# A table of places where a step's first instruction stands behind another step, an earlier copy of two columns, and one moved down unit, in a hybrid attention and convolutional-MLP layer

## The chip, the cores and the metric

The kernel runs on one NeuronCore of a Trainium2 chip. Its engines each take their instructions in the order of their own queue: TensorE (PE: matmuls and, apart, weight loads), VectorE (DVE), ScalarE (ACT), GpSimd (POOL) and SyncE (SP), which issues most of the DMAs. The metric is the device time of one execution in microseconds (us); of several executions the median counts.

## The reference

One decoder layer on x of 1024 rows by 1024 columns, in float32:

```python
h = rms_norm(x, mix_norm)
z = h @ w_in            # gq, gk, gv, gr, glr (group A), sq, sk, sv (group B)
o_gla = gla_chunked(...)            # chunked gated linear attention, 4 heads
o_gla = rms_norm(o_gla, gla_norm) * silu(gr)
o_swa = swa_sink_attention(...)     # window of 128, 8 query heads, sinks
x = x + concatenate([o_gla, o_swa]) @ w_out
h2 = rms_norm(x, ffn_norm)
u = causal_dwconv(h2 @ w_up, conv_w, conv_b)   # 3 taps, 2 x 2816 channels
a, bval = split(u, 2)
return x + (silu(a) * bval) @ w_down
```

## The kernel before

**Tiles and numbers.** The 1024 rows are 8 tiles of 128. A float32 operand is held as two parts in a type that TensorE takes at full rate, a high part (a cast, on ACT) and a low part (source minus high part, on DVE or POOL), and each product runs three passes: high by high, high by low, low by high.

**Stages.** First come the dense products with w_in by tile: queries (`dq`), keys with the gate's low-rank input (`dk`), values (`dv`), gla queries and keys (`dg`), the output gate (`dr`), all by `dense` (L389). Beside them run the two attentions. For each tile, `kvl_tr` (L475, L476) transposes the keys and the gate's input (`kpt`); ACT copies the transposed gate input to `gt`, and `kvl_la` multiplies it (`za`, L493). `swa_scores` (L525, L526) makes the window's scores (`sc`). `unit_v` ends in an ACT copy into `vg` (L920). `load_piece` brings a piece of w_in by DMA (`graw` for the g weights) and casts it in two halves (`gw`, L116). Then comes the product with w_out (`oP`, L867), the second norm, its transposes (`n2_tr`, L264) into PSUM banks `n2pt` or `fb`, and then the MLP: 22 chunks of 128 + 128 channels up (`product`, L1033), the convolution, and the way down (`dn_P`, L1214, summed into `acc` by DVE, L1218).

**Up products.** The product with w_up is a Strassen-like scheme: seven products P1 to P7 per chunk instead of eight, with weights A11, A12, S1 to S4, A22 and with operands B11, B21, B22, T1 to T4, which are halves of the transposed rows and sums of them. P1 takes A11, P2 takes A12, P3 takes S4, P5 takes S1, P6 takes S2. A product is 12 matmuls of 128x512. The sums are made in the PSUM banks of the transposes (`n2_sum`, L285 to L293) and cut into high part (`n2_part_hi`, ACT L303) and low part (`n2_part_lo`, DVE L307). The last chunks' rows of the way down go the same way by pairs of chunks: a pair has seven sums (`down_g`), 14 units of 6 matmuls (`down_pair`).

**PSUM.** Pool `psa` has four banks. The transposes of tile 6 (`n2pt_6_0`) and the up products of chunk 1 and later (`fb0` to `fb3`) share them in turn: the bank that chunk 1's P2 writes is the one that held `n2pt_6_0`, which is free only when its last reader is through. That is step `l.T4.6` in the list `STEPS`, the low part of T4 of tile 6, the last but one entry (DVE, L307).

**What sets the order.** Steps are entered with a time (`at`, `at_us`) and emitted by that time. A scheduler then orders each engine's instructions. In the stretch from the w_out product to the MLP, manual dependencies that carry no wait (`NoSync`) pin PE's instructions to the order of emission, and in its second half those of DVE, ACT and POOL too; `STEPS` is the order written out by hand for that half. Before and after that stretch the scheduler decides: chunk 0's P3, P5 and P6 come after it, and the scheduler may put them between pinned ones. A wait between engines is a semaphore.

**MLP steps.** `post` calls `c11` when P2 of a chunk is done: DVE adds P1's copy, then `conv` runs an ACT activation (first tap and bias, L1045) and two DVE taps (L1040), and `save_edge` copies the last two columns for the second half (ACT, `e`, L1089). `down_pair` units stand between products: none up to (2, 0), one behind each product up to (21, 0), then two.

Of the kernel before, what the change touches and what calls it, by code (L numbers as in the profile page):

```python
# [27 lines left out]
NPAIR = NCH // 2 - 1  # L28
# [13 lines left out]
wl.0.A22 h.T4.5 T4a.6 T4b.6 wl.0.S3 tr.7.0 copy.1 tr.7.1 b12.7 up.1.P2 l.T4.5 h.B22.7 T1.7 h.T4.6 l.B22.7  # L42
h.T1.7 T3.7 l.T1.7 h.T3.7 l.T3.7 T2.7 T4a.7 h.T2.7 T4b.7 l.T2.7 h.T4.7 l.T4.6 l.T4.7
""".split()
PASSES = ((0, 0), (0, 1), (1, 0))
HALF = (slice(0, 64), slice(64, 128))

# [2 lines left out]
def hymba_layer_kernel(ctx, tc, x, mix_norm, w_in, w_alpha2, b_alpha, gla_norm,  # L50
                       q_norm, k_norm, sinks, w_out, ffn_norm, w_up, conv_w,
                       conv_b, w_down, out):
    nc = tc.nc
# [985 lines left out]
    def tap(dst, src, w):  # L1039
        dve.scalar_tensor_tensor(dst, src, w, dst, op0=ALU.mult, op1=ALU.add)  # L1040

    def conv(ch, sd, u, y, a, z, fresh):
        ci = sd * NCH + ch
        w0, w1, w2, b = (cc[:, i, ci:ci + 1] for i in range(4))
        act.activation(u[:, a:z], y[:, a:z], AF.Identity, bias=b, scale=w2)  # L1045
        a1, a2 = (a + 1, a + 2) if fresh else (a, a)
        tap(u[:, a1:z], y[:, a1 - 1:z - 1], w1)
        tap(u[:, a2:z], y[:, a2 - 2:z - 2], w0)
# [38 lines left out]
    def save_edge(ch, key, pb):  # L1087
        e = psb[key, ch] = base.tile([P, 2], F32, tag="e", name=f"{key}_{ch}", bufs=2)
        act.copy(e, pb[:, 510:512])  # L1089

    def c11(ch):
        pb = psb["P2", ch]
        dve.tensor_add(pb, psb["p1", ch], pb)  # L1093
        ua = psb["ua", ch] = wide_tile(f"ua{ch}", "ua")
        conv(ch, 0, ua, pb, 0, 512, True)
        save_edge(ch, "e", pb)

    def c12(ch):
        pb, ua = psb["P3", ch], psb["ua", ch]
# [237 lines left out]
    for t in range(NT):  # L1337
        if t > 1:
            if t > 3:
                at(t - 2.7, load_x, t)  # L1340
                at(t - 2.5, norm1, t)
                at(t - 1.6, lambda tt=t: norm_tr(tt, xts["h", tt], "n1"))
            if t > 2:
                at(TQ + t, unit_q, t)
        at(TK + 0.6 * t, unit_k, t)
        at(TK + 0.6 * t + 1.9, kvl_tr, t)
        at(TK + 0.6 * t + 3.1, kvl_la, t)
        at(TV + t, unit_v, t)
        at(TG + t, unit_g, t)
        at(TR + t, unit_r, t)  # L1350
        if t < 4:
            at(TR + 2.05 + 0.01 * t, load_acc, t)
        else:
            at(O + 2.25 + 0.005 * t, load_acc, t)
# [110 lines left out]
    for ch, i, name in order:  # L1465
        starts[ch, i] = tu
        prods.append((ch, name, tu))
        at_us(tu, product, ch, name)
        tu += MM
        at_us(tu - 0.1, post_last if ch == L else post, ch, name)  # L1470
        if (ch, name) == (0, "P4"):
            at_us(tu - 0.05, post, 1, "P2")
        if ch < 2 or (ch, i) == (2, 0):
            n = 0
        elif ch < L - 1 or (ch, i) == (L - 1, 0):
            n = 1
        else:
            n = 2
        for _ in range(n):
            if units:  # L1480
                unit = units.pop(0)
                unit_at[unit] = tu
                at_us(tu, down_pair, *unit)
                tu += UNIT
# [9 lines left out]
    for p in range(NPAIR):  # L1494
        for k in range(7):

            n = 7 * p + k - 2
            t0 = unit_at[n // 7, n % 7, 1] + UNIT if n >= 0 else starts[1, 4 + k] if k == 0 else starts[2, 0]
            at_us(t0 + 0.02, down_w, p, k)
            at_us(t0 + 0.03, down_g, p, k)  # L1500
        for i in range(2):
            if p == 0:
                t0 = starts[1, 2 + i]
# [11 lines left out]
    for t in range(NT):  # L1515
        at_us(tu, last_row, t)
        tu += MM
    last, PINNED = {}, (mybir.EngineType.DVE, mybir.EngineType.Activation, mybir.EngineType.Pool)
    for time, _, f, a in sorted(ev, key=lambda e: e[:2]):
        n = len(nc.cur_bb.bb.instructions)  # L1520
        f(*a)
        if O <= time < TU - 0.2:
            for ins in nc.cur_bb.bb.instructions[n:]:
                e = ins.engine
# [34 lines left out]
```

## Time and profile before

| | us |
|---|---|
| median of 3 runs | 981.88 (981.22 to 982.74) |
| the profiled execution, whole | 981.06 |
| its span, first to last instruction | 979.3 |
| PE busy | 966.4 |
| DVE busy | 813.9 |
| POOL busy | 651.6 |
| ACT busy | 505.1 |

A row of the timeline gives the start, the time of the whole row, the engine, the line, the operation, output and inputs, the shape, and how many instructions follow one another without a gap; in square brackets stands the idle time before it and what ended it. Ends of matmuls are modelled and overlap the next start by some 0.16 us, so the distance of two starts is what a product costs.

### The profile page before, as it was taken

How to read it: one execution, taken by the hardware profiler on the slowest of the kernel's cores; microseconds unless marked ns; L12 is line 12 of the kernel's file. 1: busy time of each engine (PE TensorE's matmuls, PEld its weight loads, DVE VectorE, ACT ScalarE, POOL GpSimd, SP SyncE). 2: the span in 40 equal slices, each digit the busy share in tenths (PEclk: the TensorE clock that was granted, in tenths of full speed). 3: DMA queues.
4: the chain of work that ended last, by engine and by line, in shares of the span. 5: the costliest groups of instructions: out<-in, count | busy, mean ns of one | idle time of the engine just before them, and what ended most of it. 6: DMA issues, size and time to landing. Idle time of an engine off the chain costs nothing.

```text
span 979.3 us, 13946 instructions
## 1 busy us (share of the span) xinstructions
PE 966.4 (99%) x4915; PEld 839.2 (86%) x4915; DVE 813.9 (83%) x1361; ACT 505.1 (52%) x1039; POOL 651.6 (67%) x544
## 2 busy tenths in 40 slices
PE   8999999999999999999999999999999999999998
PEld 6898888888888888888888888888888888888887
DVE  6867667867656789798989899898989899998986
ACT  5637655545453487555454535455454545454441
POOL 5593123235665668777878788978878787978750
PEclk9999999999999999999999999999999999999999
DMA  7253114142204102222121211222121212122104
GB/s 230 66 142 84 44 31 118 32 88 65 99 10 150 66 22 66 64 58 72 44 86 28 77 35 57 64 65 65 44 86 44 74 35 65 44 65 64 44 22 172
DMA packets 67540, 68.23 MB, mean 70 GB/s; under 512 B 4650, under 2 KB 52237, under 8 KB 67470
## 3 DMA queue, kind: packets, MB, share of 16 engines
q1 hardware_dynamic: 63484, 62.35, 20.7%
q10 hardware_dynamic: 3986, 4.99, 2.1%
q8 instruction: 39, 0.64, 0.3%
q14 instruction: 31, 0.25, 0.1%
HBM read 58.41 MB, written 4.19 MB: 64 GB/s over the span
## 4 chain that ended last, share of the span: by engine, by line
PE 82%; DVE 8%; POOL 3%; DMA 3%; issue 2%; ACT 2%; ACTq 0%; DVEq 0%; POOLq 0%; SPq 0%
PE fb L1033 36%; PE dn_P L1214 18%; PE oP L867 7%; PE dr L389 4%; PE dg L389 4%; PE dv L389 3%; PE pv L575 1%; PE dl L1243 1%; PE fb L1243 1%; DMA qraw<-in_w_in_dram 1%; DVE ua L1040 1%; PE go L685 1%; PE ga L676 1%; PE ppt L560 1%; PE go L688 1%
## 5 line engine op out<-in xcount | busy, mean ns | idle before, releaser
L1214 PE MATMUL dn_P<-dw,dg 128*128 128x512 f32 x840 | 204.8, 381 | 1.0 <-DVE acc L1218 0.7
L1218 DVE TENSOR_TENSOR acc<-acc,dn_P 128x1024 f32<-128x1024 f32 x140 | 169.2, 1210 | 31.4 <-PE dn_P L1214 31.3
L1214 PEld LDWEIGHTS dn_P<-dw,dg 128*128 128x128 f32 x840 | 157.3, 189 | 26.7 <-DVE acc L1218 3.2
L119 POOL TENSOR_TENSOR dw<-dn,dw 128x512 fp32r<-128x512 f32 x50 | 64.4, 1289 | 37.0 <-ACT dw L116 37.0
L1040 DVE SCALAR_TENSOR_TENSOR ua<-fb,cc,ua 128x511 f32<-128x511 f32 (+1 forms) x84 | 61.8, 738 | 1.2 <-ACT ua L1045 0.8
L1033 PE MATMUL fb<-big,A11w 128*128 128x512 f32 x252 | 58.2, 379 | 1.0 <-ACT e L1089 1.0
L1033 PE MATMUL fb<-big,S1w 128*128 128x512 f32 x252 | 58.8, 379 | 0.0
L1033 PE MATMUL fb<-big,S4w 128*128 128x512 f32 x252 | 58.3, 379 | 0.0
L1033 PE MATMUL fb<-ex,S2w 128*128 128x512 f32 x252 | 58.1, 379 | 0.0
L1033 PE MATMUL fb<-big,A12w 128*128 128x512 f32 x252 | 58.1, 379 | 0.0
L1033 PE MATMUL fb<-ex,A22w 128*128 128x512 f32 x252 | 57.8, 379 | 0.0
L1033 PE MATMUL fb<-ex,S3w 128*128 128x512 f32 x252 | 57.8, 379 | 0.0
L551 POOL TENSOR_TENSOR pr<-pr,sm 128x512 f32<-128x512 f32 x16 | 17.2, 1078 | 60.8 <-DVE sm L550 34.0
L1045 ACT ACTIVATE ua<-fb,cc 128x512 f32<-128x512 f32 x42 | 32.6, 777 | 46.3 <-DVE fb L1093 29.9
L1033 PEld LDWEIGHTS fb<-big,A11w 128*128 128x128 f32 x252 | 47.6, 189 | 8.1 <-ACT e L1089 1.4
L1033 PEld LDWEIGHTS fb<-big,S4w 128*128 128x128 f32 x252 | 47.6, 189 | 7.0 <-POOL S4w L119 0.3
L1033 PEld LDWEIGHTS fb<-big,S1w 128*128 128x128 f32 x252 | 47.6, 189 | 6.8
L1033 PEld LDWEIGHTS fb<-ex,S3w 128*128 128x128 f32 x252 | 47.6, 189 | 6.8
L1033 PEld LDWEIGHTS fb<-ex,S2w 128*128 128x128 f32 x252 | 47.6, 189 | 6.8
L1033 PEld LDWEIGHTS fb<-big,A12w 128*128 128x128 f32 x252 | 47.6, 189 | 6.8
L1033 PEld LDWEIGHTS fb<-ex,A22w 128*128 128x128 f32 x252 | 47.6, 189 | 6.8
L1085 ACT COPY ca<-fb 128x512 f32<-128x512 f32 x62 | 36.3, 585 | 28.6 <-PE fb L1033 28.6
(496 smaller groups left out, 2554.9 us busy)
## 6 DMA issues: line engine op xcount, KB each, us to landing
up<-in_w_up_dram SPq DMA_DIRECT2D x44, 512.0 KB, 3.9
dn<-in_w_down_dram SPq DMA_DIRECT2D x22, 512.0 KB, 3.5
acc<-in_x_dram SPq DMA_DIRECT2D x8, 512.0 KB, 4.7
out_dram<-acc SPq DMA_DIRECT2D x15, 256.0 KB, 2.1
xt<-in_x_dram SPq DMA_DIRECT2D x7, 512.0 KB, 3.3
vraw<-in_w_in_dram SPq DMA_DIRECT2D x4, 512.0 KB, 4.3
graw<-in_w_in_dram SPq DMA_DIRECT2D x4, 512.0 KB, 3.6
qt<-qt ACTq DMA_DIRECT2D x16, 128.0 KB, 2.2
```

Of the source, the lines that this page charges most:

```text
L119: (eng or pool).tensor_sub(lo, src, hi.bitcast(F32))
L389: pe.matmul(pb[:, :n], lhsT=big[:, t, k, ra, :], rhs=two_streams(ws[k][:, rb, :n]), start=(k == 0 and i == 0), stop=(k == KD - 1 and i == 2))
L551: pool.tensor_tensor(pr, pr, den[:, hs].rearrange("p (j o) -> p j o", o=1).broadcast_to((P, 4, P)), ALU.mult)
L560: pe.transpose(pb[:, j * P:(j + 1) * P], pr[:, j], ident)
L867: pe.matmul(pb, lhsT=left[:, k, ra, :], rhs=two_streams(ow[name, k][:, rb, :]), start=(onto is None and k == 0 and n == 0), stop=(k == 3 a ...
L1033: pe.matmul(pb, lhsT=w[:, ra, k, :], rhs=b_operand(bn, k, rb).rearrange("p t (h c) -> p t c h", h=2), start=(onto is None and i == 0), sto ...
L1040: dve.scalar_tensor_tensor(dst, src, w, dst, op0=ALU.mult, op1=ALU.add)
L1045: act.activation(u[:, a:z], y[:, a:z], AF.Identity, bias=b, scale=w2)
L1085: act.copy(dst, pb)
L1214: pe.matmul(pb[:, i], lhsT=g[:, ra, c:c + P], rhs=two_streams(w[:, rb, :]), start=(onto is None and n == 0), stop=(n == 2), skip_group_che ...
L1218: dve.tensor_add(acc, acc, pb.rearrange("p i (c h) -> p i h c", h=2))
L1243: pe.matmul(pb[:, c0:c1], lhsT=g[:, ra, (t % 4) * P:(t % 4 + 1) * P], rhs=two_streams(w[:, rb, c0:c1]), start=(ch == NCH - 2 and i == 0), ...
```

## The change

Line numbers in the changed kernel are 4 to 6 higher than before: `product` is L1037 instead of L1033, `n2_tr` L268 instead of L264, `n2_part_lo` L311 instead of L307, `swa_scores` L529 and L530, `dense` L393, the casts of weights L120, `vg` L924.

Four edits:

1. A table `BEHIND` names steps by engine. The loop that emits the steps records the instructions of each step by engine, and ties the first instruction of a step in the table behind one of another step's (its last, -1, or first, 0) with a dependency that carries no wait. For `load_piece.g.0.512.3` that is the first cast of the piece alone.
2. `conv` takes a function that it calls right behind its activation; `c11` passes `save_edge`, so that the copy of the two columns comes ahead of the DVE taps, in all chunks.
3. `kvl_tr(1)` has the time 3.05 behind TK instead of 2.5.
4. Behind the second product of the last chunk stands one down unit instead of two, and the sums `down_g(9, 1)` of the last pair have another time.

```diff
+BEHIND = {("PE", "kvl_tr.1"): ("unit_k.5", -1), ("PE", "swa_scores.1.0"): ("unit_v.1", -1),
+          ("Activation", "load_piece.g.0.512.3"): ("unit_v.7", -1), ("PE", "product.0.P3"): ("step.up.1.P2", -1),
+          ("PE", "product.0.P5"): ("product.0.P3", -1),
+          ("PE", "product.0.P6"): ("product.0.P5", -1), ("DVE", "down_g.9.1"): ("post.20.P2", 0)}
...
-    def conv(ch, sd, u, y, a, z, fresh):
+    def conv(ch, sd, u, y, a, z, fresh, then=None):
...
         act.activation(u[:, a:z], y[:, a:z], AF.Identity, bias=b, scale=w2)
+        if then:
+            then()
...
-        conv(ch, 0, ua, pb, 0, 512, True)
-        save_edge(ch, "e", pb)
+        conv(ch, 0, ua, pb, 0, 512, True, lambda: save_edge(ch, "e", pb))
...
-        at(TK + 0.6 * t + 1.9, kvl_tr, t)
+        at(TK + (3.05 if t == 1 else 0.6 * t + 1.9), kvl_tr, t)
...
-        elif ch < L - 1 or (ch, i) == (L - 1, 0):
+        elif ch < L - 1 or (ch, i) in ((L - 1, 0), (L - 1, 1)):
...
-            at_us(t0 + 0.03, down_g, p, k)
+            at_us((starts[L - 1, 1] + MM - 0.08 if (p, k) == (NPAIR - 1, 1) else t0) + 0.03, down_g, p, k)
...
+        key, mine = ".".join([f.__name__] + [str(v) for v in a if isinstance(v, (int, str))]), {}
+        for ins in nc.cur_bb.bb.instructions[n:]:
+            mine.setdefault(ins.engine.name, []).append(ins)
+        for e, group in mine.items():
+            places[e, key] = [ins.name for ins in group]
+            if (e, key) in BEHIND:
+                other, i = BEHIND[e, key]
+                tc.add_manual_dep(group[0], places[e, other][i], mybir.DependencyInfo(
+                    mybir.DependencyClass.NoSync, mybir.DependencyReason.DATA), reason="order of the program")
```

**First place: PE, where the last transposes meet the first up products.** Before, these rows follow one another on PE. `fb_4095` and `fb_4106` with `ident` are the transposes of tile 7; S4w, S1w and S2w are the weights of chunk 0's P3, P5 and P6, written to the banks `gb`; `fb_4202` from A12w_4136 is P2 of chunk 1, the step `up.1.P2`, into the bank that held `n2pt_6_0`:

```order
L264 MATMUL fb_4095<-ident,n2h_4111 128x128 x4
L264 MATMUL fb_4106<-ident,n2h_4111 128x128 x4
L1033 MATMUL gb_4248<-big,S4w_4046 128x512 x12
L1033 MATMUL gb_4261<-big,S1w_4139 128x512 x12
L1033 MATMUL gb_4115<-ex_3141,S2w_4157 128x512 x12
L1033 MATMUL fb_4202<-big,A12w_4136 128x512 x12
```

And these in the changed kernel, on the same engine at the same place:

```order
L268 MATMUL fb_4095<-ident,n2h_4111 128x128 x4
L268 MATMUL fb_4106<-ident,n2h_4111 128x128 x4
L1037 MATMUL fb_4202<-big,A12w_4136 128x512 x12
L1037 MATMUL gb_4248<-big,S4w_4046 128x512 x12
L1037 MATMUL gb_4261<-big,S1w_4139 128x512 x12
L1037 MATMUL gb_4115<-ex_3141,S2w_4157 128x512 x12
```

P2 of chunk 1 moved ahead of chunk 0's P3, P5 and P6, and stands right behind the transposes. Its first matmul waits on DVE for the last reader of its bank. DVE's rows there are the same in both kernels but for the line numbers; in the changed one, `ex_3518` from `n2pt_0_4056` is `l.T4.6`, that last reader, and `fb_4202` from `early` is the sum that needs the product:

```order
L295 TENSOR_TENSOR fb_4095<-big,fb_4106 128x4x2x64
L297 TENSOR_TENSOR fb_4095<-fb_4095,big 128x4x2x64
L1044 SCALAR_TENSOR_TENSOR ua_4242<-gb_4141,cc,ua_4242 128x511
L311 TENSOR_TENSOR ex_3141<-fb_4106,ex_3141 128x4x128
L311 TENSOR_TENSOR ex_3518<-n2pt_0_4056,ex_3518 128x4x128
L311 TENSOR_TENSOR ex_3518<-fb_4095,ex_3518 128x4x128
L1044 SCALAR_TENSOR_TENSOR ua_4242<-gb_4141,cc,ua_4242 128x510
L1099 TENSOR_TENSOR fb_4202<-early,fb_4202 128x512
```

On DVE only the last of these rows moved, ahead of sums of chunk 0 that followed the tap before.

**Second place: PE between two value products.** Before, `sc_0_0_1387` are the scores of tile 1, `za_1338` is the gate's product of a later tile, and `dv_1358` is the value product of tile 1:

```order
L475 MATMUL kpt_1345<-ident,kn_1126 128x128
L476 MATMUL kpt_1345<-ident,gn_1121 96x128
L525 MATMUL sc_0_0_1387<-kt,qt_1277 128x256
L526 MATMUL sc_0_0_1387<-kt,ql_1278 128x256
L525 MATMUL sc_0_0_1387<-kt,qt_1277 128x256
L526 MATMUL sc_0_0_1387<-kt,ql_1278 128x256
L493 MATMUL za_1338<-wa,gt_1244 128x256
L389 MATMUL dv_1358<-vw_793,big 128x512 x3
```

In the changed kernel the scores follow the end of the value product (its last two groups are shown):

```order
L393 MATMUL dv_1358<-vw_1150,big 128x512 x3
L393 MATMUL dv_1358<-vw_1153,big 128x512 x3
L529 MATMUL sc_0_0_1387<-kt,qt_1277 128x256
L530 MATMUL sc_0_0_1387<-kt,ql_1278 128x256
L529 MATMUL sc_0_0_1387<-kt,qt_1277 128x256
L530 MATMUL sc_0_0_1387<-kt,ql_1278 128x256
```

The four score matmuls moved from ahead of `za_1338` to behind all of `dv_1358`.

**Third place: ACT ahead of the last value copy.** Before, the two casts from `graw_2028`, the last piece of the g weights, stand ahead of `vg`:

```order
L116 CAST gw_1996<-graw_1994 128x512
L116 CAST gw_1999<-graw_1994 128x512
L116 CAST gw_2030<-graw_2028 128x512
L116 CAST gw_2033<-graw_2028 128x512
L920 ACTIVATE vg<-dv_1903,rn 128x512
```

In the changed kernel, on ACT:

```order
L120 CAST gw_1996<-graw_1994 128x512
L120 CAST gw_1999<-graw_1994 128x512
L120 CAST gw_2033<-graw_2028 128x512
L924 ACTIVATE vg<-dv_1903,rn 128x512
L120 CAST gw_2030<-graw_2028 128x512
```

The first of the two casts moved behind `vg`; the second, from the same DMA, stayed ahead of it.

More of the change, by code (lines that the diff above doesn't have):

```diff
@@ L1517, in hymba_layer_kernel @@
         tu += MM
-    last, PINNED = {}, (mybir.EngineType.DVE, mybir.EngineType.Activation, mybir.EngineType.Pool)
+    places, last, PINNED = {}, {}, (mybir.EngineType.DVE, mybir.EngineType.Activation, mybir.EngineType.Pool)
     for time, _, f, a in sorted(ev, key=lambda e: e[:2]):
```

## The prediction

> **What bounds the kernel now.** I began with the page: busy time by engine, and the granted clock by slice.
>
> ```profile
> PE 966.4 (99%) x4915; PEld 839.2 (86%) x4915; DVE 813.9 (83%) x1361; ACT 505.1 (52%) x1039; POOL 651.6 (67%) x544
> PEclk9999999999999999999999999999999999999999
> ```
>
> PE is busy for 966.4 of 979.3 us; the other 12.9 are the most that any new order can win, and they hold the start and the end of the program too. So I went to PE's waits, and then to windows of the MLP.
>
> ```profile
> PE sc L525 <- ACT vg L920: 1.5, 1, 1.5
> PE dg L389 <- ACT vg L920: 1.4, 1, 1.4
> PE fb L1033 <- ACT e L1089: 1.0, 1, 1.0
> PE kpt L475 <- DVE kn L466: 0.9, 1, 0.9
> PE gb L1033 <- ACT big L303: 0.8, 1, 0.8
> PE dn_P L1214 <- DVE acc L1218: 0.7, 1, 0.7
> ```
>
> ```profile
> 450.00:500.00 50.00, 50.00 (x233) 43.49 (x232) 47.59 (x61) 25.42 (x43) 43.28 (x32) 1.00 0.18 55
> 850.00:900.00 50.00, 50.00 (x233) 43.49 (x232) 45.59 (x56) 25.26 (x43) 40.25 (x31) 1.00 0.21 64
> 900.00:920.00 20.00, 19.03 (x88) 16.05 (x87) 19.93 (x24) 8.59 (x16) 15.75 (x12) 1.00 0.14 40
> ```
>
> The first number behind the colon is the window, the second PE's busy time. Each wait in the list happens once, and all six sum to 6.3 us. From 450 on, PE has no gap up to the last pair: in both whole windows it is busy for 50.00 of 50. Two things follow. The edits can win at most these 6.3 us. And whatever delays PE ahead of the MLP reaches the end undiminished, as there is no slack behind it but the 0.97 us in 900 to 920.
>
> **Part 1: chunk 0's P3, P5 and P6 behind chunk 1's P2.** This place decides. First PE:
>
> ```profile
> 376.22 1.04 PE L264 MATMUL fb<-ident,n2h 128*128 128x128 f32 x8
> 378.04 2.86 PE L1033 MATMUL gb<-big,S4w 128*128 128x512 f32 x12 [0.78 <-ACT big L303]
> ...
> 386.13 2.75 PE L1033 MATMUL fb<-big,A12w 128*128 128x512 f32 x12
> 410.73 2.86 PE L1033 MATMUL fb<-big,A11w 128*128 128x512 f32 x12 [1.00 <-ACT e L1089]
> ```
>
> Then the DVE rows that lead to the release of the bank into which A12w's product goes, the window around them (its fourth column is DVE), and two ACT casts among them:
>
> ```profile
> 377.61 0.67 DVE L307 TENSOR_TENSOR ex<-n2pt,ex 128x512 fp32r<-128x512 f32 x1
> ...
> 384.06 0.68 DVE L307 TENSOR_TENSOR ex<-fb,ex 128x512 fp32r<-128x512 f32 x1
> 384.66 0.68 DVE L307 TENSOR_TENSOR ex<-n2pt,ex 128x512 fp32r<-128x512 f32 x1
> ```
>
> ```profile
> 376.20:385.40 9.20, 8.42 (x42) 7.00 (x41) 9.07 (x16) 5.96 (x11) 6.13 (x6) 1.00 0.57 171
> ```
>
> ```profile
> 382.80 1.32 ACT L303 CAST ex<-fb 128x512 fp32r<-128x512 f32 x2 [1.41 <-DVE fb L291]
> ```
>
> The transposes of tile 7 end at 376.22 + 1.04 = 377.26. Before, S4w, S1w and S2w came next, after 0.78 us, and PE met A12w at 386.13. The bank that this product writes is released by the DVE row at 384.66, which ends at 385.34; PE came 0.8 us after that, and so no wait shows. Now A12w stands next behind the transposes. From 377.61 to 385.34 DVE has one instruction after another, some 0.60 us apart (384.06 to 384.66; busy for 9.07 of 9.20 us in the window), and none of them needs one of the three products that moved back: they make the sums of tile 7 in the transposes' banks. So the release cannot come earlier because PE is idle, and its place in DVE's order has not changed.
>
> PE then starts A12w at 385.34 + 0.06 = 385.40 (0.06 is what lies between an ACT cast's end and the S4w product's start before). It waits 8.14 us in place of 0.78. From S4w's start to chunk 2's first product (A11w at 410.73 less its wait of 1.00) PE has 409.73 - 378.04 = 31.69 us of work, the same products in both kernels but in another order. The new one ends at 385.40 + 31.69 = 417.09. The wait of 1.00 for `e` should be gone by then: the edge copy stands ahead of the taps, and the first half's sum is done with A12w, early. That is 417.09 - 410.73 = **+6.4 us**. Behind it the down unit now stands ahead of A22w of chunk 1 and needs a DVE cut that comes at about the same time; I cost it at nothing, as A22w needed the same sums before, with 0.5 us as the upper end.
>
> **A slower restart.** An idle time of 8 us on PE is nowhere in this trace. The nearest rows are the first matmuls:
>
> ```profile
> 1.67 2.50 PE L1285 MATMUL warm<-warm,tri 128*128 128x512 f32 x5 [1.67 <-DVE warm L148]
> 3.97 2.27 PE L1293 MATMUL mix<-mix,tri 128*128 128x512 f32 x4
> 2.00:4.00 2.00, 2.00 (x6) 1.37 (x5) 1.74 (x3) 0.97 (x3) 1.94 (x9) 1.00 0.89 292
> ```
>
> The five matmuls take 3.97 - 1.67 = 2.30 us, 0.46 each, where twelve of this shape take 2.59 (386.13 to the next product), 0.216 each. The granted clock of that window reads 1.00 all the same, so the column does not show it. If PE starts slowly after 8 us as it does after the launch, the five alone cost 5 x 0.244 = 1.2 us, and with the four of the next row, at 0.57 each, 2.6. Bounds: 0 and 2.6. I take 1.9, midway between the two counts, since nine in a row were slow: **+1.9**. The Trainium skill, TensorE: Matmul & The Clock Gate, section on the HAM clock gate, says that PE's clock falls to half after an idle window of about 3.4 us and returns after about as much sustained work. By that the restart would cost about 1.7 us, an estimate from that page; the early rows agree in the pitch, and the clock column does not.
>
> **Part 2: `kvl_tr(1)` behind the sixth key product.**
>
> ```profile
> 73.57 0.33 PE L475 MATMUL kpt<-ident,kn 128*128 128x128 f32 x1 [0.89 <-DVE kn L466]
> 77.04 0.39 PE L493 MATMUL za<-wa,gt 128*128 128x256 f32 x1
> 76.73 0.26 ACT L487 CAST gt<-kpt 96x128 fp32r<-96x128 f32 x1 [1.11 <-DVE kl L482]
> ```
>
> The 0.89 us goes, but a little later stands `za` at 77.04, right behind its ACT cast (76.73 + 0.26 = 76.99). That cast hangs on tile 0's own chain and not on what moved. PE arrives 0.89 earlier and waits there. I take **0**, with -0.9 and +0.8 as ends: the moved transposes delay tile 1's own cast and `za`, and DVE and ACT work closely there.
>
> **Part 3: the scores behind the value product.**
>
> ```profile
> 93.14 0.38 PE L525 MATMUL sc<-kt,qt 128*128 128x256 f32 x1 [1.50 <-ACT vg L920]
> 93.82 5.34 PE L389 MATMUL dv<-vw,big 128*128 128x512 f32 x24
> 92.39 0.69 ACT L920 ACTIVATE vg<-dv,rn 128x512 f32<-128x512 f32 x1
> 93.23 0.25 ACT L487 CAST gt<-kpt 96x128 fp32r<-96x128 f32 x1
> ```
>
> PE waited for `vg`, and then the value product stood behind a `za` that needs the cast at 93.23. In the new order that cast goes ahead of `vg`, to about 92.39: 0.84 earlier, and the product starts near 92.84 instead of 93.82. But the four scores (93.14 to 93.68) now run behind it: 0.98 - 0.54 = **-0.4**. Ends: -1.5, the whole wait, and 0, as ACT is the engine that is late here.
>
> **Part 4: one cast behind `vg`.**
>
> ```profile
> 149.05 1.14 ACT L116 CAST gw<-graw 128x512 fp32r<-128x512 f32 x2 [1.87 <-DMA graw<-in_w_in_dram]
> 150.09 0.68 ACT L920 ACTIVATE vg<-dv,rn 128x512 f32<-128x512 f32 x1
> 150.82 5.45 PE L389 MATMUL dg<-gw,big 128*128 128x512 f32 x24 [1.42 <-ACT vg L920]
> ```
>
> ACT waits 1.87 us for the DMA with both casts ahead of `vg`. One of them stays there, with the same wait. So only one cast's pitch is saved, (150.09 - 149.05) / 2 = 0.52: **-0.5**, with -1.4 and 0 as ends. The cast that moved is used late in the 24 matmuls of `dg`.
>
> **Part 5: the last pair, and the edge copies.**
>
> ```profile
> 911.91 1.53 PE L1214 MATMUL dn_P<-dw,dg 128*128 128x512 f32 x6 [0.23 <-ACT ca L1085]
> 914.61 1.56 PE L1214 MATMUL dn_P<-dw,dg 128*128 128x512 f32 x6 [0.74 <-DVE acc L1218]
> 905.60 1.65 DVE L1196 TENSOR_TENSOR D<-D,ub 128x512 f32<-128x512 f32 x1
> 907.18 1.76 DVE L1197 TENSOR_TENSOR ub<-ub,ub 128x512 f32<-128x512 f32 x1
> 387.57 0.17 ACT L1089 COPY e<-gb 128x2 f32<-128x2 f32 x1
> ```
>
> The waits of 0.23 and 0.74 hang on DVE, which is late by the pair's sums at 905.60 and 907.18. With the sums behind chunk 20's P2 addition and one unit fewer before P6, I take **-0.8**, ends -1.0 and 0. The edge copies keep their number and 0.17 us each on ACT, which is half idle; the one wait on `e` is counted above, so 0.
>
> **The sum**, against the profiled execution: 981.06 + 6.4 + 1.9 + 0 - 0.4 - 0.5 - 0.8 = 987.7 us. That execution was 0.8 us below the median of the runs shown, 981.88. I say **987.5**, about 0.6% slower.
>
> **Rivals.**
> - *The stall without the slow restart.* The clock column speaks for it: 1.00 in every window. 987.7 - 1.9 = 985.8. By the page named above the restart would be slow. Chance 0.27, against 0.55 for the forecast.
> - *Faster: the release of A12w's bank comes soon.* All other waits go, and A12w starts with its transposes: 981.06 - 0.8 - 1.0 - 0.4 - 0.5 - 0.8 = 977.6. Price and point: every microsecond of the release is a microsecond of PE. The sum is zero when the release ends 4.7 us earlier, at 380.7, and the slow restart stays away: (380.7 + 0.06 - 377.26) - 0.78 - 1.0 - 1.7 = 0. Against it stands that DVE has no gap in which to be faster there. Chance 0.07; near that point, within 0.2% of before, 0.06.
> - *More waits follow.* DVE loses work while PE stands still: the sums of chunk 0 need the third product behind the stall, which ends near 385.40 + 3 x 2.6 = 393. If DVE then trails PE, the unit of the 0.5 us above and the next ones wait too, 2 to 4 us more: about 990 to 992. For it: DVE busy for 47.59 of 50 us at 450. Against: PE's own delay gives DVE the same time. Chance 0.05.
>
> **The range.** The low end is the stall without the restart and with larger gains of parts 3 to 5, 985.8 less some 2.3; the high end the sum with 2.6 for the restart and the upper ends of the small terms, with part of the last rival: 983.5 to 991.5. A measurement of this kernel tells about 0.2%, some 2 us, from no change. Faster 0.07, within 0.2% 0.06, slower 0.87.
>
> **What would show it.** In the profile after, the largest of PE's waits should be A12w at L1037 on DVE L311, some 8 us near 377 to 385; the products behind it should follow without gaps, and the next few 128x512 matmuls should stand 0.43 us or more apart if the restart is slow. The waits on `e` and on `dn_P` should be gone, that on `vg` at 150 be 0.9. I am wrong if A12w starts before 381, if PE is found idle in 450 to 900, or if the scores and key places lose more than they win.

## The result and the profile after

| | us, median (range, executions) | ratio to before, 95% interval |
|---|---|---|
| before, same chip | 981.75 (981.04 to 982.74, 6) | 1 |
| after | 994.48 (989.97 to 996.34, 6) | 1.0122 [1.0099, 1.0146] |

The change makes the kernel 1.2% slower, some 12 us, where 0.6% was forecast and 991.5 was the upper end. The profiled execution took 996.34 us, with a span of 994.6. It is the slowest of the six, so what is taken from it is some 2 us above the typical case.

PE's longest waits in the changed kernel (total us, times, longest), without the one at the program's start:

```profile
PE fb L1037 <- DVE ex L311: 8.1, 1, 8.1
PE dn_P L1219 <- DVE acc L1223: 3.4, 4, 1.1
PE fb L1037 <- POOL A11w L123: 2.3, 1, 2.3
PE za L497 <- ACT gt L491: 1.9, 3, 1.2
PE sc L530 <- DMA ql<-ql: 1.0, 1, 1.0
PE dg L393 <- ACT vg L924: 1.0, 1, 1.0
```

PE's rows around the place of part 1, in order of time (start, us):

```profile
377.59 1.04 PE L268 MATMUL fb<-ident,n2h 128*128 128x128 f32 x8
386.77 4.50 PE L1037 MATMUL fb<-big,A12w 128*128 128x512 f32 x12 [8.15 <-DVE ex L311]
...
422.64 2.42 PE L1037 MATMUL fb<-big,A11w 128*128 128x512 f32 x10 [2.25 <-POOL A11w L123]
```

The windows (behind the colon PE, then PEld, DVE, ACT, POOL, and the granted clock):

```profile
378.00:388.00 10.00, 1.85 (x9) 1.43 (x8) 9.84 (x16) 5.43 (x11) 7.33 (x7) 0.77 0.36 105
388.00:400.00 12.00, 12.00 (x52) 10.31 (x52) 1.69 (x3) 2.45 (x5) 2.46 (x3) 0.91 0.13 45
450.00:900.00 450.00, 446.48 (x2060) 387.85 (x2059) 422.83 (x518) 220.33 (x381) 365.56 (x270) 1.00 0.19 58
900.00:950.00 50.00, 50.00 (x233) 43.80 (x232) 47.45 (x63) 25.68 (x44) 43.96 (x33) 1.00 0.18 53
```

Four things are to be seen. The forecast stall is there, 8.15 us on the row that was named. The twelve matmuls behind it take 4.50 us instead of 2.75, and now the granted clock is below 1.00 there: 0.77 and 0.91. But PE, which was never idle from 450 to 900 before, now loses 3.52 us there, most of it in three waits of about 1 us on `acc`; and the first product of chunk 2, A11w, waits 2.25 us on POOL where it waited 1.00 on `e`. The last pair's waits are gone: 50.00 of 50 in 900 to 950. So the stall, the slow restart and the last pair came as forecast, and two things that were costed at nothing did not: the start of chunk 2 and the stretch from 450 to 900.

### The profile page after: what moved, and what is told of

Same layout as the page of the kernel before. It is cut to its first block, busy times and chain, and to the rows that moved or that the text cites. A ratio compares the mean times of both kernels' runs of the same rounds, so it can differ in the third digit from the quotient of the medians.

```text
span 994.6 us, 13961 instructions
## 1 busy us (share of the span) xinstructions
PE 969.8 (98%) x4915; PEld 841.3 (85%) x4915; DVE 829.4 (83%) x1361; ACT 502.6 (51%) x1039; POOL 654.1 (66%) x544
## 4 chain that ended last, share of the span: by engine, by line
PE 76%; DVE 13%; POOL 4%; issue 3%; DMA 3%; ACT 2%; ACTq 0%; POOLq 0%; DVEq 0%; SPq 0%
PE fb L1037 31%; PE dn_P L1219 16%; PE oP L871 7%; PE dr L393 4%; PE dg L393 4%; PE dv L393 3%; DVE acc L1223 2%; DVE ua L1044 1%; PE pv L579 1%; DVE dg L123 1%; PE dl L1248 1%; PE fb L1248 1%; DVE ub L1202 1%; PE go L689 1%; PE ga L680 1%
## 5 line engine op out<-in xcount | busy, mean ns | idle before, releaser
L123 POOL TENSOR_TENSOR dw<-dn,dw 128x512 fp32r<-128x512 f32 x50 | 69.7, 1394 | 35.7 <-ACT dw L120 35.7
L1037 PE MATMUL fb<-big,A12w 128*128 128x512 f32 x252 | 59.7, 387 | 8.1 <-DVE ex L311 8.1
L1037 PEld LDWEIGHTS fb<-big,A12w 128*128 128x128 f32 x252 | 48.7, 194 | 15.5 <-DVE ex L311 8.4
L1037 PE MATMUL fb<-big,A11w 128*128 128x512 f32 x252 | 58.2, 379 | 2.3 <-POOL A11w L123 2.3
L1037 PE MATMUL fb<-ex,S2w 128*128 128x512 f32 x252 | 58.3, 379 | 0.0
L1037 PE MATMUL fb<-big,S1w 128*128 128x512 f32 x252 | 58.3, 379 | 0.0
L1037 PE MATMUL fb<-ex,S3w 128*128 128x512 f32 x252 | 58.1, 379 | 0.0
L1037 PE MATMUL fb<-ex,A22w 128*128 128x512 f32 x252 | 58.0, 379 | 0.0
L1037 PE MATMUL fb<-big,S4w 128*128 128x512 f32 x252 | 57.8, 379 | 0.0
L1037 PEld LDWEIGHTS fb<-big,A11w 128*128 128x128 f32 x252 | 47.6, 189 | 9.4 <-POOL A11w L123 2.7
L1037 PEld LDWEIGHTS fb<-big,S1w 128*128 128x128 f32 x252 | 47.6, 189 | 6.8
L1037 PEld LDWEIGHTS fb<-ex,S2w 128*128 128x128 f32 x252 | 47.6, 189 | 6.8
L1037 PEld LDWEIGHTS fb<-big,S4w 128*128 128x128 f32 x252 | 47.6, 189 | 6.8
L1037 PEld LDWEIGHTS fb<-ex,A22w 128*128 128x128 f32 x252 | 47.6, 189 | 6.8
L1037 PEld LDWEIGHTS fb<-ex,S3w 128*128 128x128 f32 x252 | 47.6, 189 | 6.8
L1071 ACT ACTIVATE ub<-fb,cc 128x512 f32<-128x512 f32 x42 | 32.6, 777 | 35.0 <-PE fb L1037 19.0
```

The source lines that it names most:

```text
L123: (eng or pool).tensor_sub(lo, src, hi.bitcast(F32))
L1037: pe.matmul(pb, lhsT=w[:, ra, k, :], rhs=b_operand(bn, k, rb).rearrange("p t (h c) -> p t c h", h=2), start=(onto is None and i == 0), sto ...
L1071: act.activation(u, y, AF.Identity, bias=b, scale=w2)
```

## The experiments

Every kernel was timed in five rounds beside the kernel before on the same chip. "Ratio" is to that kernel, with its 95% interval; it need not be the quotient of the two medians. "PE lost" is PE's idle time in one profiled execution.

### 1. The three product entries alone, and the change without them

```
no_products:    BEHIND without ("PE", "product.0.P3"), ("PE", "product.0.P5"), ("PE", "product.0.P6")
only_products:  the kernel before, with these three entries alone
no_attention:   the change without the entries of kvl_tr.1, swa_scores.1.0 and load_piece.g.0.512.3
                (kvl_tr at its old time)
```

> The change without its three product entries; all other edits stay. Theory: the stall of 8.1 us, the slow restart (1.75), the wait of 2.3 us for A11w of chunk 2 and the small waits of PE on DVE's sums between 450 and 900 (about 3.4 us) all hang on these entries and go. Left are about +0.6 us from the three attention entries and -1 us from the last pair: 980.5 to 982.5 us, PE busy for 50.00 of 50 us in the windows from 450 to 900. Rival: the small waits in the MLP come from the edge copies, the only instructions whose order differs in chunks 3 to 19; then 984 to 986 us and PE idle for 3 us between 450 and 900.

> The kernel before with the three product entries alone: no other edit. Theory: 7.4 (stall) + 1.75 (slow restart) + 2.3 - 1.0 (A11w of chunk 2 waits for its weights instead of the edge copy) + about 3 (small waits on DVE's sums) = 13 us more than before, 993 to 996 us. Rival (edge copies make the small waits): 990 to 992 us, with PE busy for 50.00 of 50 us from 450 on.

> The change without its entries for kvl_tr, swa_scores and load_piece and with kvl_tr(1) at its old time; the product entries and the other edits stay. Theory: the three together lose about 0.6 us by the trace, so 993 to 995 us, and PE's waits of 1.5 (scores), 1.4 (dg) and 0.9 (kpt) us are back. Rival: they win the 0.9 us that I had forecast, so this kernel is about 1 us slower than the change, 995 to 997 us.

| | median | ratio | wait of A12w | wait of A11w | PE lost in 450 to 900 |
|---|---|---|---|---|---|
| no_products | 984.35 | 1.0008 [0.9995, 1.0021] | none | 1.06 | 2.05 |
| only_products | 995.35 | 1.0128 [1.0108, 1.0149] | 8.17 | 1.82 | 0 |
| no_attention | 996.52 | 1.0135 [1.0117, 1.0154] | 8.14 | 2.19 | 1.31 |

The three entries carry the loss by themselves. Without them the ratio is that of before within what can be told, though the median is 2.0 us above that of before in the same rounds (982.33). There the rival came true: 984 to 986 us, with PE idle between 450 and 900. only_products came to the 993 to 996 us of its theory, but without the 3 us of small waits that stood in that sum. The profile places only part of what came instead: a restart that cost 0.9 us more, 5.44 for the twelve matmuls. The three attention entries together show nothing beside the 12 us: with them 1.0122, without them 1.0135, and the intervals overlap. The forecast's 0.9 us fits that as well as none.

In the kernel with the products alone, PE:

```profile
389.48 5.44 PE L1036 MATMUL fb<-big,A12w 128*128 128x512 f32 x12 [8.17 <-DVE ex L310]
426.03 2.43 PE L1036 MATMUL fb<-big,A11w 128*128 128x512 f32 x10 [1.82 <-POOL A11w L122]
```

So the longer wait of A11w belongs to the products as well.

### 2. The bank's release earlier on DVE

```
-... h.T4.6 l.B22.7
-h.T1.7 ... h.T4.7 l.T4.6 l.T4.7
+... h.T4.6 l.B22.7 l.T4.6                       (release_early)
+h.T1.7 ... h.T4.7 l.T4.7
+... T4b.6 h.T4.6 wl.0.S3 tr.7.0 l.T4.6 copy.1   (release_first)
```

> The change with step l.T4.6, the last reader of the bank that A12w's product waits for, moved from the last place but one in the list of steps to behind l.B22.7, ten steps earlier; nothing else. Theory: the release comes some 5 us earlier, PE waits about 2.5 to 3 us there instead of 8.1; and if the slow restart is PE's clock after a long idle time, it goes too, with the granted clock at 1.00: 7 to 10 us faster than the change, 984 to 987 us. Rival for the slow restart (the product itself is slow at this place, for its operands or for other engines' traffic): the wait shrinks in the same way, but A12w still takes about 4.3 us instead of 2.6.

> The change with both steps h.T4.6 and l.T4.6 right behind the sums they read, still ahead of tile 7's own steps: the earliest that the sums allow. By the rows of release_early the bank is free some 1.1 us sooner, so PE waits about 1.8 us for it instead of 2.9. Theory (the slow product is PE's clock, which drops after an idle time somewhere between 1.5 and 2.15 us, as dg shows: 1.42 us and full speed, 2.15 us and 1.7 us lost): this wait is between the two, and either A12w takes 2.6 us with the granted clock at 1.00 and the kernel comes to 982 to 984 us, or it takes 4.3 us with the clock under 1 and comes to 984.5 to 986. Rival (the product is slow here for another reason): 4.3 us with the clock at 1.00.

release_early: 986.63, ratio 1.0045 [1.0029, 1.0061]. release_first: 987.37, 1.0048 [1.003, 1.0067]. A12w in the one and in the other:

```profile
380.12 4.54 PE L1037 MATMUL fb<-big,A12w 128*128 128x512 f32 x12 [2.89 <-DVE ex L311]
```

```profile
379.45 2.86 PE L1037 MATMUL fb<-big,A12w 128*128 128x512 f32 x12 [1.83 <-DVE ex L311]
```

The wait follows DVE's order of the release, as the forecast's sum has it: moved forward, it falls from 8.15 to 2.89 and 1.83 us, and the time falls by 7 to 8. The slow restart did not go with it in the first: after only 2.89 us of idle time the twelve matmuls still take 4.54, and the granted clock from 378 to 384 is 0.72. After 1.83 they take 2.86, and it is 1.00: so the place itself is not slow.

release_first missed its 982 to 984 us by 3 us and more. Its shorter wait and fast restart gained nothing over release_early; in the profiles PE lost 2.27 us in 450 to 900 there, and 0.16 in release_early. Neither kernel is as fast as the one before: the rest of the change still costs.

### 3. The other parts alone

```
only_edge:  conv(ch, 0, ua, pb, 0, 512, True, lambda: save_edge(ch, "e", pb))   and nothing else
only_last:  BEHIND = {("DVE", "down_g.9.1"): ("post.20.P2", 0)}, with its two lines on times
only_load:  BEHIND = {("Activation", "load_piece.g.0.512.3"): ("unit_v.7", -1)}
```

> The kernel before with the earlier edge copies alone. Theory: the copies put DVE's first tap of each chunk behind one more ACT instruction, and that makes the single waits of about 1 us on DVE's sums between 450 and 900 which the change, no_products and no_attention show and before and only_products don't: PE idle for 1 to 3 us there, 983 to 985 us. Rival: the waits come with the shift in time that other edits make, not with the copies: PE busy for all of 450 to 900, the wait of 1.0 us for e at 410 gone or replaced by one on a tap, 981 to 982.5 us.

> The kernel before with the last pair's sums and the moved down unit alone. Theory: the two waits on the last pair (0.23 and 0.74 us) go, 0.5 to 1.0 us faster than before, ratio 0.9990 to 0.9995. Rival: the sums that now come later make a wait of the same size behind them, ratio 1.0000.

> The kernel before with the entry for load_piece alone (one cast behind vg). Theory: PE's wait at dg falls by one cast, from 1.4 to about 0.9 us, and in executions where the DMA lands late (2.2 us of waiting in only_products and no_attention) it stays under the point where the clock drops, so that the 1.7 us lost there go too: executions with a mean clock under 0.999 become rare, median 0.5 to 1.5 us lower than before. Rival: qt and ql are issued later behind the moved cast and the scores wait for them (0.4 to 1.0 us in the change, no_products and release_early), so that nothing is won: ratio 1.000.

| | median | ratio | PE lost in 450 to 900 |
|---|---|---|---|
| only_edge | 984.87 | 1.0029 [1.0017, 1.0042] | 1.34 |
| only_last | 980.54 | 0.998 [0.997, 0.9989] | 0 |
| only_load | 981.98 | 0.9994 [0.9985, 1.0002] | 0 |

The surprise is the first: twenty-odd ACT copies of 0.15 us, made earlier, cost 2.8 us by themselves. only_last gained about 2 us, more than the 0.5 to 1.0 of its theory, and only_load decides between neither of its two. In 450 to 900 only_edge starts 2072 matmuls, the kernel before 2081; nine are worth 9 x 0.216 = 1.9 us. It has a wait that the kernel before has nowhere in that stretch:

```profile
806.46 1.53 PE L1215 MATMUL dn_P<-dw,dg 128*128 128x512 f32 x6 [1.21 <-DVE acc L1219]
```

The change without them settles whose the losses in 450 to 900 are:

> The whole change, but with the edge copies at their old place. Theory A, the small waits of PE in 450 to 900 come with the earlier edge copies: no wait of dn_P on acc of 0.9 us or more is left in 450 to 900, PE is busy for 50.00 in each window of 50 there, and the time is that of the change less some 2.8 us, about 991.5 (ratio 1.008 to 1.011). The stall of 8.1 us and the slow restart stay. Theory B, they come from DVE's arrears behind the stall: the waits stay, 993.5 to 995 (ratio 1.012 to 1.013).

no_edge: 991.9, ratio 1.0099 [1.0084, 1.0114], and PE busy for the whole of 450 to 900:

```profile
450.00:900.00 450.00, 450.00 (x2082) 391.94 (x2081) 412.82 (x521) 224.56 (x382) 371.79 (x274) 1.00 0.19 60
```

They come with the copies, not with DVE's arrears behind the stall: in the five kernels so far with the copies at their old place (before, only_products, no_edge, only_last, only_load) PE loses nothing in 450 to 900, with the stall of 8.1 us or without; in the six with early copies it loses from 0.16 (release_early) to 3.52 us.

### 4. Why early copies cost: DVE and POOL

The copies are not on DVE at all. The two kernels differ in the time of DVE's instructions whose two input tensors both lie in SBUF, the engines' on-chip memory, and not in a PSUM bank. First the short ones, in the kernel before, DVE and then POOL, in order of time:

```profile
598.60 0.66 DVE L1040 SCALAR_TENSOR_TENSOR ua<-e,cc,ua 128x2 f32<-128x2 f32 x1
601.63 0.24 DVE L1073 TENSOR_TENSOR ub<-ua,ub 128x2 f32<-128x2 f32 x1
```

```profile
597.96 1.28 POOL L119 TENSOR_TENSOR A12w<-up,A12w 128x512 fp32r<-128x512 f32 x1
600.56 1.29 POOL L984 TENSOR_TENSOR up<-up 128x512 f32<-128x512 f32 x1
```

The same two instructions in the kernel with the early copies alone:

```profile
599.96 1.27 DVE L1040 SCALAR_TENSOR_TENSOR ua<-e,cc,ua 128x2 f32<-128x2 f32 x1
607.21 1.18 DVE L1075 TENSOR_TENSOR ub<-ua,ub 128x2 f32<-128x2 f32 x1
```

```profile
599.94 1.28 POOL L119 TENSOR_TENSOR S2w<-up,S2w 128x512 fp32r<-128x512 f32 x1 [0.58 <-ACT S2w L116]
607.09 1.28 POOL L119 TENSOR_TENSOR S3w<-up,S3w 128x512 fp32r<-128x512 f32 x1 [1.32 <-ACT S3w L116]
```

A product of two columns takes 0.24 us or 1.18. Add each row's time to its start: 598.60 + 0.66 = 599.26 and POOL's 597.96 + 1.28 = 599.24; 599.96 + 1.27 = 601.23 and 599.94 + 1.28 = 601.22; 607.21 + 1.18 and 607.09 + 1.28 likewise. Each ends when the POOL instruction beside it ends. In the kernel before, between 450 and 910, all 43 of DVE's single rows `ua<-e` and `ub<-ua,ub`, of one or two columns, that last over 0.4 us end within 0.1 us of the end of a POOL row, and none of the 25 shorter ones lies wholly under one. So these instructions do not run beside POOL; they wait for it, for whatever is left of its 1.3 us. What that is depends on the moment at which they meet. The Trainium skill says so, SBUF — State Buffer, section "Who interferes with whom": a DVE instruction with two inputs in SBUF contends with a GpSimd instruction that reads SBUF, and with at most one such input it does not. The trace agrees in both halves: the taps from `fb`, which read a PSUM bank and one SBUF tensor, take 0.73 to 0.76 us wherever they stand.

The groups of `ub<-ua,ub` in 450 to 900 (busy time and mean ns behind the first bar) and DVE's idle time ahead of `acc` (behind the second), of before and of after:

```profile
L1218 DVE TENSOR_TENSOR acc<-acc,dn_P 128x1024 f32<-128x1024 f32 x116 | 140.3, 1210 | 28.4 <-PE dn_P L1214 28.4
L1073 DVE TENSOR_TENSOR ub<-ua,ub 128x2 f32<-128x2 f32 x32 | 14.7, 460 | 0.0
```

```profile
L1223 DVE TENSOR_TENSOR acc<-acc,dn_P 128x1024 f32<-128x1024 f32 x114 | 138.0, 1210 | 17.4 <-PE dn_P L1219 17.4
L1079 DVE TENSOR_TENSOR ub<-ua,ub 128x2 f32<-128x2 f32 x34 | 23.2, 681 | 0.0
```

The mean rises from 460 to 681 ns and DVE's reserve falls from 28.4 to 17.4 us. But this alone does not make PE wait: in release_early the mean is 704 ns, and PE loses 0.16 us in 450 to 900. The waits of about 1 us hang on a longer instruction of the same kind: the cut that makes the low part of `dg`, an operand of the way down, of 128x512, behind a one-column tap. DVE and POOL in the kernel before:

```profile
786.72 1.02 DVE L1040 SCALAR_TENSOR_TENSOR ua<-e,cc,ua 128x1 f32<-128x1 f32 x1
787.67 0.68 DVE L119 TENSOR_TENSOR dg<-ub,dg 128x512 fp32r<-128x512 f32 x1
787.81 1.68 POOL L1182 TENSOR_TENSOR dn<-dn 128x512 f32<-128x512 f32 x1
```

And with the early copies alone, ahead of the wait at 806.46:

```profile
788.96 1.26 DVE L1040 SCALAR_TENSOR_TENSOR ua<-e,cc,ua 128x1 f32<-128x1 f32 x1
790.14 1.84 DVE L119 TENSOR_TENSOR dg<-ub,dg 128x512 fp32r<-128x512 f32 x1
790.15 1.29 POOL L119 TENSOR_TENSOR dw<-dn,dw 128x512 fp32r<-128x512 f32 x1
```

Both times the tap is held to the end of a POOL row, and the cut follows. Before, the cut starts 0.14 us ahead of POOL's next instruction and takes 0.68; POOL's takes 1.68 in place of 1.28. With the early copies another POOL row stands over the tap, the next one starts within 0.01 us of the cut and goes first, and the cut takes 1.16 us longer. PE's wait is 1.21. This pair of tap and cut stands 48 times in 450 to 900 in those six kernels with early copies: the cut took 1.84 or 1.85 us in 9 places, and these 9, and no other, were followed by a wait of 0.9 us or more on `acc`. In the kernels with the copies at their old place (the five, and load_last of section 5) it took 0.68 in all 52.

To test it, DVE's short instructions were written so that only one tensor operand lies in SBUF, with the same values:

```
-        tap(u[:, 0:1], e[:, 1:2], cc[:, 1, ci:ci + 1])
-        tap(u[:, 0:2], e[:, 0:2], cc[:, 0, ci:ci + 1])
+        w0, w1 = cc[:, 0, ci:ci + 1], cc[:, 1, ci:ci + 1]
+        for j, k, w in ((0, 1, w1), (0, 0, w0), (1, 1, w0)):
+            dve.tensor_scalar(u[:, j:j + 1], e[:, k:k + 1], w, u[:, j:j + 1], op0=ALU.mult, op1=ALU.add)
...
-        dve.tensor_mul(u[:, 0:2], ua[:, 0:2], u[:, 0:2])
+        for j in range(2):
+            dve.tensor_scalar(u[:, j:j + 1], ua[:, j:j + 1], u[:, j:j + 1], None, op0=ALU.mult)
```

> The kernel before with the earlier edge copies alone, and DVE's two-column products and edge taps, whose tensors both lie in SBUF, written as one-column instructions with one such tensor and a scalar per partition (the same values). Theory A, DVE's two-column instructions are held until the POOL instruction beside them ends, and the earlier copies only shift which of them are hit: the one-column instructions take 0.3 us at most, none ends with a POOL row, the waits of dn_P on acc of about 1 us in 450 to 900 are gone, and the time is 981.5 to 982.8 (ratio 0.999 to 1.0005), against 984.87 for the copies alone. Theory B, the copies cost by the tap that waits behind the copy or by ACT's order: the waits stay, 984 to 985.5 (ratio 1.002 to 1.004). Some of DVE's and ACT's instructions trade places with their neighbours in this kernel, for one instruction becomes two.

only_edge_one: 978.23 (978.04 to 980.16), ratio 0.9963 [0.995, 0.9975]. That is 6.6 us less than with the copies alone, and less than the kernel before. Two of the one-column instructions in a row, the POOL instruction over them, and their group in 450 to 900:

```profile
599.74 0.32 DVE L1077 TENSOR_SCALAR ub<-ua,ub 128x1 f32<-128x1 f32 x2
```

```profile
598.87 1.28 POOL L984 TENSOR_TENSOR up<-up 128x512 f32<-128x512 f32 x1
```

```profile
L1077 DVE TENSOR_SCALAR ub<-ua,ub 128x1 f32<-128x1 f32 x66 | 11.3, 201 | 0.0
```

They begin and end under a POOL instruction, which no two-column product did. The one-column tap ahead of the cut takes 0.26 or 0.27 us at all nine places, and tap and cut together 1.62 to 1.64 (1.70 before, 3.10 at the place shown with the early copies). PE:

```profile
450.00:900.00 450.00, 450.00 (x2086) 394.05 (x2085) 406.97 (x588) 227.59 (x381) 375.40 (x276) 1.00 0.19 59
900.00:950.00 50.00, 50.00 (x233) 43.77 (x233) 44.73 (x61) 24.99 (x44) 37.85 (x28) 1.00 0.10 32
```

PE has no gap, and in the same 450 us it starts 2086 matmuls; the kernel before, also busy for 450.00, started 2081. The five are worth 5 x 0.216 = 1.1 us: PE loses bits to waiting too short to be listed, which its busy time does not show. This kernel gained more than expected for that reason and because the wait of A11w halves to 0.57 and those of the last pair (0.97) go. One reservation: as one instruction became two, some of ACT's and DVE's casts changed places with their neighbours, so not all of the 6.6 us need be the collisions. Nor was the kernel before timed with the one-column form and nothing else; the next section has it with two other edits.

### 5. Combinations

> The kernel before with the cast behind the last value copy and with the last pair's sums and its down unit moved. If the two add up as they were measured apart (0.6 and 2.0 us): 979.5 to 980.3, ratio 0.997 to 0.998. If PE's wait at dg, 1.75 us in the run of the cast alone, drops the clock in most executions: 980.5 to 981.5, ratio 0.9985 to 0.9995.

> The same with DVE's two-column instructions written with one SBUF tensor each. If the collisions with POOL also set the end of the last pair, another 0.3 to 0.9 us less: about 979.3, ratio 0.9965 to 0.9975. If PE is the bound there and the instructions, now more of them, only take DVE's time: as load_last or up to 0.5 us more, ratio 0.9975 to 0.9985.

> The whole change, with DVE's two-column instructions written with one SBUF tensor each. If what the time has beyond the stall, the slow restart and the last pair comes from DVE's two-column instructions held by POOL: no wait of dn_P on acc of 0.9 us or more in 450 to 900, the stall of 8.1 us and a slow first product (4.3 us or more) as before, and a time of 987.5 to 989 (ratio 1.0055 to 1.007). If A11w's wait of 2.25 us comes from POOL held by DVE, it shrinks to 1.1 or less; if from its slot, in which a product is read that now ends later, it stays at 1.8 or more. If the waits in 450 to 900 come from arrears behind the stall: they stay, 991 to 993 (ratio 1.009 to 1.011).

> The change without its three product entries, with DVE's two-column instructions written with one SBUF tensor each. If the waits behind the earlier edge copies were all that its other parts lost: no wait of dn_P on acc of 0.9 us or more in 450 to 900, 977 to 978.3 (ratio 0.995 to 0.996), at or below both kernels of this kind. If the attention entries lose on their own: 978.5 to 980 (ratio 0.9965 to 0.998).

| | edit | median | ratio |
|---|---|---|---|
| load_last | before, with `load_piece` and the last pair | 980.2 | 0.9983 [0.9973, 0.9993] |
| load_last_one | the same, one SBUF operand | 978.51 | 0.9963 [0.9951, 0.9976] |
| no_products_one | the change less the products, one SBUF operand | 979.45 | 0.9969 [0.9957, 0.998] |
| after_one | the whole change, one SBUF operand | 992.33 | 1.0105 [1.0089, 1.0121] |

The cast adds nothing measurable to the last pair. With one SBUF operand three kernels beat both the kernel before and the change, at 978 to 979.5; the parts of the change that are in them make no difference that can be told. What the form itself wins is clear of noise on two kernels with early copies, only_edge (1.0029 to 0.9963) and no_products (1.0008 to 0.9969); on load_last (0.9983 to 0.9963) and on the whole change (1.0122 to 1.0105) the intervals overlap. after_one came out above its 987.5 to 989: the waits in 450 to 900 went (PE busy for 450.00), but PE waits behind the stall as before, now at three places, and the restart cost more:

```profile
385.84 5.49 PE L1037 MATMUL fb<-big,A12w 128*128 128x512 f32 x12 [8.13 <-DVE ex L311]
421.77 0.67 PE L1037 MATMUL fb<-big,A11w 128*128 128x512 f32 x2 [1.57 <-ACT dw L120]
422.93 2.42 PE L1037 MATMUL fb<-big,A11w 128*128 128x512 f32 x10 [0.49 <-POOL A11w L123]
429.71 2.86 PE L1037 MATMUL fb<-big,S1w 128*128 128x512 f32 x12 [1.33 <-DVE ub L1079]
```

The two waits of A11w sum to 2.06 us, against 2.25 in the change. So A11w's wait does not come from the collisions. What it hangs on is read from ACT, POOL and SyncE's queue (SPq). First before, then after:

```profile
399.28 0.34 SPq L1175 DMA_DIRECT2D dn<-in_w_down_dram  x1
401.92 0.62 ACT L116 CAST A11w<-up 128x512 fp32r<-128x512 f32 x1 [1.85 <-PE fb L1033]
404.58 0.62 ACT L116 CAST dw<-T 128x512 fp32r<-128x512 f32 x1 [0.95 <-POOL T L1183]
```

```profile
404.51 6.75 SPq L950 DMA_DIRECT2D up<-in_w_up_dram  x2
411.35 0.53 SPq L1180 DMA_DIRECT2D dn<-in_w_down_dram  x1
416.35 1.27 POOL L1188 TENSOR_TENSOR T<-dn,dn 128x512 f32<-128x512 f32 x1 [4.25 <-DMA dn<-in_w_down_dram]
417.66 0.62 ACT L120 CAST dw<-T 128x512 fp32r<-128x512 f32 x1 [2.35 <-POOL T L1188]
418.18 0.61 ACT L120 CAST A11w<-up 128x512 fp32r<-128x512 f32 x1
421.33 1.26 POOL L123 TENSOR_TENSOR A11w<-up,A11w 128x512 fp32r<-128x512 f32 x1
```

Before, A11w's cast stands ahead of the cast from `T` on ACT; after, it stands behind it, and `T` waits on POOL for a down weight's DMA. That DMA starts at 411.35, before at 399.28. It writes the place in SBUF that held chunk 0's weights A22w, so it stands behind that product, which the stall and the new order delay from 396.49 to 406.74. The other 1.8 us come from SyncE's order: after, the issue stands behind that of an `up` weight (the second of the two in the row, at 410.89), which waits for POOL's low part of S3w. This chain is read from the profile and was not tested: no kernel has that cast moved back.

## Why the forecast was too low

- **Part 1, the stall: right.** Forecast 8.14 us in place of 0.78, measured 8.13 to 8.17 in five kernels. It moved with DVE's release, and DVE's order sets it.
- **The slow restart: right in kind, and its rival fell.** Forecast 1.9; the twelve matmuls take 4.50 in place of 2.75, 1.75 more, and from 1.6 to 2.7 more in the five kernels with this stall. The forecast weighed against it that the clock column reads 1.00 at the launch; here the column shows it (0.77, 0.91). The forecast's estimate of 1.7 us from the Trainium skill, TensorE: Matmul & The Clock Gate, section on the HAM clock gate, agrees with the 1.75 and not with the 2.7.
- **"The wait of 1.00 for `e` should be gone", and nothing in its place: this step failed.** The wait on `e` went, but A11w waits 2.25 us for its weights, and a later down unit waits 0.34 at 434: 2.6 where 0 was forecast. The reason given was wrong too. The early edge copy does not clear the place: alone (only_edge) it leaves A11w waiting 1.08 on a DVE tap instead of 1.00 on `e`; with the stall and the copies at their old place (only_products, no_edge) the wait on `e` is gone all the same, and A11w waits 1.82 for its weights. The forecast looked at the sums that PE's next products need, and not at ACT's casts, whose order had changed there, nor at the down DMA that starts behind a delayed product. The unit ahead of A22w, costed "at nothing, with 0.5 us as the upper end", did wait for nothing (at 414.62). "More waits follow", at 0.05, came true only in part: PE waits behind the stall, but on ACT, POOL and a DMA rather than on DVE.
- **Part 5, the edge copies at 0: this step failed as well.** Alone they cost 0.29% [0.17, 0.42], about 2.8 us; in the change the medians with and without them differ by 2.6 us, though the intervals overlap (1.0122 against 1.0099). "ACT is half idle" was true and beside the point: what moved was the moment at which DVE meets POOL, and DVE at 47.59 busy of 50 had little to give. PE idle in 450 to 900 was one of the forecast's own signs of being wrong. How a copy on ACT shifts that moment was not followed link by link. Shown is that the losses come with the copies, that each wait of about 1 us follows a cut of `dg` held by POOL, and that these waits are gone when the short instructions have one SBUF operand.
- **The attention parts, forecast -0.9 in sum: neither shown nor excluded.** The wait of the scores for `vg` went, but three waits of `za` (1.9 in all) and one of the scores on the DMA of `ql` (1.0) came in its place. The last transposes start 1.37 us later than before in this execution (377.59 against 376.22), but 0.43 earlier in no_edge (375.79), which has the same entries. The cast alone gives 0.9994, which can't be told from 1.
- **The last pair, forecast -0.8: right in direction and mechanism.** The waits of 0.23 and 0.74 are gone. Timed alone it gives -0.2% [-0.3, -0.11], 1.1 to 2.9 us; the profile places only the 0.97.

In the two profiled executions the 15.3 us between the spans (994.6 and 979.3) come to this: 1.4 by the last transposes; then 7.4 for the stall, 1.75 for the restart, 2.25 for A11w and 0.34 for the unit less the 1.0 for `e`, 10.7 in all; 21 matmuls fewer in 450 to 900 (2060 against 2081), 4.5; less 1.0 for the last pair. The sum is 15.6. Timed by themselves, the parts give about what was measured: products +1.28%, copies +0.29%, last pair -0.2%, cast -0.06%, together +1.31% against 1.22%, with intervals of 0.1 to 0.2% each. The products' 1.28% are 12.6 us where part 1 and the restart came to 8.3, so at least as much was missing there as at the copies. The forecast named where PE would stop, and took for free what it could not see in PE's waits: the order of the casts behind the stall, and the moment at which two other engines meet.

A slip made the forecast lower still: its sum is 6.6 us above the profiled execution, and 6.6 above the median of 981.88 would be 988.5, not 987.5. That too lies below the 994.48 measured.

## What to carry to other kernels

Before a product is moved ahead on PE, look up the place of its bank's last reader in the other engine's order: here the reader's delay was lost in full, as PE had no slack behind it, and the casts and DMAs that start behind the delayed products were late with it. Where an engine is as busy beside a full PE as DVE here (412.70 of 450 us), do not take an edit on its neighbours as free: read the same instruction's time in several places, and where it varies several times over, find whose rows it ends with, and follow the chain from a wait of PE back to the row that grew. Short DVE instructions with two SBUF operands beside a busy POOL are worth trying with a per-partition scalar; here that won 6.6 us on the early copies alone, and nothing clear of noise in the whole change.

## What the runs showed of the hardware

- DVE's instructions with two tensors in SBUF are held to the end of a POOL instruction that reads SBUF, if that one started first: short ones of 0.17 to 0.27 us become up to 1.33, a cut of 128x512 goes from 0.68 to 1.85. If DVE starts first, POOL's 1.28 us become 1.68 or 1.80. At the cut of `dg` the two starts lay within 0.03 us of each other where POOL won. A one-column instruction with one such tensor and a scalar per partition takes 0.19 to 0.27 us under a running POOL instruction; two or three of them stand for one.
- PE's clock can drop after short idle times. The Trainium skill, TensorE: Matmul & The Clock Gate, section on the HAM clock gate, has about 3.4 us for it; the runs show less. After 2.89 us twelve matmuls of 128x512 took 4.54 us instead of 2.75. At the `dg` product the 24 took 7.13 us in place of 5.45 after 2.15 and 2.22 us, and 19 of them 6.02 in place of 4.37 after 1.75:

```profile
152.28 6.02 PE L390 MATMUL dg<-gw,big 128*128 128x512 f32 x19 [1.75 <-ACT vg L921]
152.00:154.00 2.00, 1.72 (x4) 1.45 (x5) 1.72 (x4) 1.46 (x5) 1.19 (x1) 0.56 0.83 245
```

  (the kernel with the cast alone; 0.56 is the granted clock). After 1.83 us in release_first, 2.05 us at `dg` in no_products_one and 2.25 us at A11w in the changed kernel it stayed at 1.00. So between 1.75 and 2.25 us it went either way, and each drop in this range, and that after 2.89, cost 1.65 to 1.8 us. No run here tells what decides it. Transposes stand ahead of all of these idle times but the 2.25, where products of 128x512 stand on both sides; whether that matters was not tested.
- A PE that is busy for all of a window can still be slower than it could be: 2081 matmuls or 2086 in the same 450.00 us.
